# Two heads side by side on TensorE, and mask adds behind the first block, in a two-block transformer kernel

## The chip, the cores and the metric

One core of a Trainium2 chip. The metric is the device time of one execution in microseconds, as the median of several runs. Engines: TensorE (PE, matmul), VectorE (DVE), ScalarE (ACT), GpSimd (POOL) and SyncE (SP, which here only issues DMAs).

## What is computed

Two blocks of a decoder at a batch of 1, a sequence of 256 and a width of 1024, in fp32. Block 1 has two layers; each mixes with dilated attention (three groups of four heads of 64; the groups of a head slot are merged by their softmax denominators) and with stick-breaking attention, and then runs a convolution FFN of width 2816:

```python
h = rms_norm(x, norm_mix[l]); proj = h @ w_in[l]
sc = jnp.einsum('bqhd,bqkhd->bhqk', qg, kg) * scale        # dilated, per group, masked
p = jnp.exp(sc - m); o = jnp.einsum('bhqk,bqkhd->bqhd', p, vg) / den
...
up = h @ w_up; a, bval = up[..., :D_FF], up[..., D_FF:]
a = causal_depthwise_conv(a, conv_w) + conv_b
x = x + (jax.nn.silu(a) * bval) @ w_down
```

Block 2 has a layer with an even mixer (differential attention, and sparse attention that an indexer's scores select), one with an odd mixer (attention with sinks and a relative bias), cross-attention to a memory in both, and an MLP. The relative bias comes from a table of 32 buckets; some of the biases get a mask added.

## The kernel before, in words

Big matmuls (L231) take weights in two fp32r parts: SP loads a block of 512 KB of raw weights (L195, three buffers, up to five blocks ahead), ACT copies each half of it to the high part (L201), DVE subtracts to get the low part (L202), and PE multiplies in three terms. Every weight half on PE therefore needs one DVE instruction, which stands in DVE's queue among all the rest.

Attention runs in pairs of heads of 64, so that one head uses one half of the array. `dil_pair` (L721) takes one pair of head slots: the scores of three groups go to two banks, one per head (L734, buffers `sd`), once for the first 128 queries and in two banks for the second; DVE adds the mask and takes the maximum (L738); the transposed weights pass through PE and ACT (L749 to L754); and the values are summed over the groups into one bank, whose two halves belong to the two heads (L759 for the first 128 keys, L763 for the others, `pvd`). In block 2 `score_banks` (L580) makes the scores of two heads in two banks (L585, L586, `sc`), for the indexer, differential, sparse and odd-mixer pairs; `pv_pair` (L519) does their values (L524, L525, `pv`), for the odd mixer, the sparse pairs and the cross-attention.

The relative bias passes through DRAM: in the FFN of the first layer, seven copies of 768 KB (L654, buffer `skew_d`) are issued on POOL's queue, one for each step j = 2 to 8, paced by a small copy (L888) behind that step's product (L886). `bias_tile` (L489) loads a bias tile from there (L487, on POOL's queue, three buffers) and, where a mask is given, adds it on DVE (L494). The tiles are loaded as early as the pool lets them, long before block 2.

The order of instructions on each engine is decided by a scheduler that simulates the program when the kernel is built: it follows data, buffers and the `no_sync` edges. Such an edge says only that one instruction stands behind another in the order, and adds no semaphore.

Of the kernel before, what the change touches and what calls it, by code (L numbers as in the profile page):

```python
# [130 lines left out]
def net(ctx, tc, A, out):  # L131
# [86 lines left out]
    def hold(on):  # L218

        i = state["n"]  # L220
        if not on:
            state["limit"] = len(W)
            if i:
                ahead()
            return
        while i < len(W) and W[i][0] == W[state["n"]][0]:
            i += 1
        state["limit"] = i

# [259 lines left out]
    def bias_tile(heads, mask=None):  # L489
        t = sb("bias", "bias", (len(heads), T))  # L490
        for j, h in enumerate(heads):
            bias_load(t[:, j], h)
        if mask is not None:
            dve.tensor_tensor(t, t, mask[:, None, :].to_broadcast([P, len(heads), T]), op=OP.add)  # L494
        return t
# [5 lines left out]
    def lay_p(p, n1):  # L501
# [14 lines left out]
        act.activation(s1, t1, AF.Copy)  # L516
        return s0, s1

    def pv_pair(s0, s1, v, n1):  # L519

        o = bank("pv", "pv", (T,))
        for h in range(2):
            oo = o[h * 64:h * 64 + 64]
            pe.matmul(oo, v(h, 0), s0[:, h], start=True, stop=False, skip_group_check=True)  # L524
            pe.matmul(oo[:, T - n1:], v(h, 1), s1[:, h], start=False, stop=True, skip_group_check=True)  # L525
        return o
# [131 lines left out]
    for l in range(DEPTH):  # L658
# [62 lines left out]
        def dil_pair(hp):  # L721

            ps_p = []
            for i in range(2):
# [5 lines left out]
                for b, gs in enumerate(banks):  # L730
                    s = [bank("sc", "sd", (len(gs), n)) for _ in range(2)]
                    for g in gs:
                        for m in range(2):
                            pe.matmul(s[m][:, g - gs[0]], half(qT[g], hp, m)[:, col(i)], half(kT[g], hp, m)[:, :n],  # L734
                                      start=(g == gs[0]), stop=True, skip_group_check=True)
                    w = slice(gs[0], gs[-1] + 1)
                    for m in range(2):
                        dve.tensor_tensor_reduce(pv[m][:, w], s[m], m_dil[:, w, T - n:], 1.0,  # L738
                                                 mx[m][:, 0:1] if b else -3e38, op0=OP.add, op1=OP.max,
                                                 accum_out=mx[m][:, b:b + 1])  # L740
# [8 lines left out]
            for m in range(2):  # L749
                for dst, i, kt in ((t0[m][:, :, 0:P], 0, 0), (t0[m][:, :, P:T], 1, 0), (t1[m], 1, 1)):  # L750
# [89 lines left out]
        def residual(w, y, k, gains):  # L840
# [5 lines left out]
            def on_part(c, a, b):  # L846
# [3 lines left out]
                dve.tensor_tensor(t, x[c // 2][:, c % 2], a, op=OP.add)  # L850
# [90 lines left out]
    for j in range(2):  # L941
        dve.tensor_tensor_reduce(lprod, lamv[:, 2 * j], lamv[:, 2 * j + 1], 1.0, 0.0, op0=OP.mult, op1=OP.add,
                                 accum_out=lsum[:, j:j + 1])
# [79 lines left out]
    def even(h, nrm):  # L1023
# [48 lines left out]
        def index_scores(hp):  # L1072
            s = score_banks(lambda m: half(qi[hp // 2], hp % 2, m), lambda m: half(kc, 0, m))
            for hh in range(2):
                hd = 2 * hp + hh
                r = sb("ft", "relu", (384,))
                act.activation(r, s[hh], AF.Relu)
# [32 lines left out]
        def diff_pair(hp):  # L1110
            pl, dens = [], []
            for hh in range(2):
# [5 lines left out]
                for n, c in enumerate(COLS):  # L1118
                    m, i = n // 2, n % 2
                    dve.tensor_tensor_reduce(p[:, c], s[m][:, TILE[i]], bt[:, T - (i + 1) * P:], 1.0, -3e38,  # L1120
                                             op0=OP.add, op1=OP.max, accum_out=mx[:, n:n + 1])
# [30 lines left out]
        def dsa_pair(hp):  # L1152
# [10 lines left out]
            for n, c in enumerate(COLS):  # L1163
                dve.tensor_tensor_reduce(p[:, c], s[n // 2][:, TILE[n % 2]], bs[:, n // 2, TILE[n % 2]], 1.0, -3e38, op0=OP.add,  # L1164
                                         op1=OP.max, accum_out=mx[:, n:n + 1])
# [18 lines left out]
    def odd(h, nrm):  # L1184
# [22 lines left out]
        def pair(ch):  # L1207
# [7 lines left out]
            for n, cc in enumerate(cols):  # L1215
                m, i = n // 2, n % 2
                dve.tensor_tensor_reduce(p[:, cc], s[m][:, TILE[i]], bt[:, m, T - (i + 1) * P:], 1.0, -3e38,
                                         op0=OP.add, op1=OP.max, accum_out=mx[:, n:n + 1])
# [281 lines left out]
```

## Time and profile before

| | us |
|---|---|
| median of 3 runs | 1460.91 (1459.95 to 1466.13) |
| profiled execution | 1462.57 |
| its span on the core | 1460.5 |
| PE busy in the span | 1404.1 |
| DVE busy | 1015.4 |
| ACT busy | 886.0 |
| POOL busy | 34.2 |

The mean granted clock of PE was 0.988. The span is one execution of the profiled core; 2.1 us lie around it, and the execution is 1.66 us longer than the median. A row of PE's timeline is a run of instructions of one line: its start, its width, and in brackets the idle time before it and what released it. The small matmuls in fp32 leave two records each, so x4 in a row of them means two instructions. A row's end is modelled and may overlap the start of the next.

### The profile page before, as it was taken

To read this page: it belongs to the slowest core of one execution; us is meant where nothing else is said; L and a number is where in the kernel's file an instruction comes from. 1 tells how busy PE (TensorE), PEld (TensorE's weight loads), DVE (VectorE), ACT (ScalarE), POOL (GpSimd) and SP (SyncE) were. 2 spreads that over 40 slices of the span, in tenths; PEclk is the share of its full clock that TensorE was granted. 3 is DMA by queue.
4 is the path that set the end of the run, shared out by engine and by line. 5 is a ranking of instruction groups with operands and counts; after the bars stand their busy time and mean duration, and the time that the engine had idled before them with its cause. 6 is when DMAs were issued, how large, how long until landed. Compare 5 with 4: busy or idle time off the path is not lost.

```text
span 1460.5 us, 26250 instructions
## 1 busy us (share of the span) xinstructions
PE 1404.1 (96%) x9948; PEld 1274.4 (87%) x9948; DVE 1015.4 (70%) x2135; ACT 886.0 (61%) x1744; POOL 34.2 (2%) x63
## 2 busy tenths in 40 slices
PE   8999999799999999999999998899999999899997
PEld 6789999798888899999999987699989978699986
DVE  6555887567665659888867795687656876677554
ACT  7556665455565566666756656576656676576553
POOL 1000000100000000000000010000000010000000
PEclk9999999899999999999999999999999999999998
DMA  8533666576654345565665554156566534266662
GB/s 263 166 116 106 186 187 213 175 227 198 199 173 147 102 151 178 186 187 186 207 196 160 156 158 132 61 157 186 182 183 185 167 102 131 62 199 188 188 188 87
DMA packets 74447, 241.62 MB, mean 165 GB/s; under 512 B 11663, under 2 KB 16159, under 8 KB 74321
## 3 DMA queue, kind: packets, MB, share of 16 engines
q1 hardware_dynamic: 67568, 230.03, 50.8%
q0 software_dynamic: 6608, 9.74, 2.2%
q8 instruction: 78, 1.28, 0.4%
q14 instruction: 49, 0.39, 0.1%
q10 hardware_dynamic: 144, 0.19, 0.0%
HBM read 238.79 MB, written 6.60 MB: 168 GB/s over the span
## 4 chain that ended last, share of the span: by engine, by line
PE 85%; DMA 6%; DVE 4%; ACT 4%; issue 1%; SPq 0%; POOL 0%; DVEq 0%; ACTq 0%; POOLq 0%
PE mm L231 52%; PE mw L231 21%; DMA raw<-in_wt_dram 4%; PE ssum L427 2%; PE mo L231 1%; DVE w L202 1%; PE sd L734 1%; DMA skew_d<-brel_d 1%; ACT w L201 1%; PE pT L483 1%; PE pv L524 1%; PE sc L586 1%; PE sc L585 1%; PE pv L525 1%; PE pTd L483 1%
## 5 line engine op out<-in xcount | busy, mean ns | idle before, releaser
L202 DVE TENSOR_TENSOR w<-raw,w 128x512 fp32r<-128x512 f32 (+2 forms) x866 | 585.2, 685 | 336.2 <-ACT w L201 327.2
L201 ACT ACTIVATE w<-raw 128x512 fp32r<-128x512 f32 (+2 forms) x866 | 532.2, 625 | 424.4 <-PE mm L231 218.1
L231 PE MATMUL mm<-xh,w 128*128 128x256 f32 x5892 | 723.6, 283 | 20.5 <-DVE fa L885 13.4
L231 PEld LDWEIGHTS mm<-xh,w 128*128 128x128 f32 x5892 | 704.2, 189 | 37.4 <-issue 20.1
L231 PE MATMUL mw<-xh,w 128*128 128x512 f32 (+1 forms) x1832 | 329.3, 340 | 4.6 <-DVE mx L1164 2.5
L231 PEld LDWEIGHTS mw<-xh,w 128*128 128x128 f32 x1832 | 282.1, 189 | 47.7 <-DVE mx L1164 2.9
L231 PE MATMUL mm<-w,xh 128*128 128x512 f32 (+2 forms) x672 | 147.1, 372 | 7.2 <-ACT w L201 7.1
L231 PEld LDWEIGHTS mm<-w,xh 128*128 128x128 f32 x672 | 114.0, 191 | 30.7 <-ACT w L201 8.1
L978 ACT ACTIVATE xh<-x,vec 128x256 fp32r<-128x256 f32 x48 | 22.6, 501 | 11.5 <-DVE x L1333 11.0
L487 POOL DMA_DIRECT2D bias<-skew_d x28 | 15.1, 543 | 611.7 <-DVE nm L535 275.0
L880 ACT ACTIVATE ftt<-fa,vec 128x256 f32<-128x256 f32 x44 | 24.1, 595 | 8.1 <-DVE fa L875 6.9
L231 PE MATMUL mo<-xh,w 128*128 128x256 f32 x192 | 28.0, 288 | 0.5 <-ACT xh L498 0.5
L231 PEld LDWEIGHTS mo<-xh,w 128*128 128x128 f32 x192 | 24.4, 189 | 3.8 <-issue 1.2
L981 DVE SCALAR_TENSOR_TENSOR xh<-x,vec,xh 128x256 fp32r<-128x256 f32 x48 | 22.0, 480 | 1.1 <-ACT xh L978 1.1
L431 ACT ACTIVATE sq<-x 128x512 f32<-128x512 f32 x33 | 20.4, 618 | 2.4 <-DMA x<-in_xT_dram 2.1
L881 DVE SCALAR_TENSOR_TENSOR ftt<-fa,vec,ftt 128x255 f32<-128x255 f32 x44 | 20.9, 483 | 0.7
L882 DVE SCALAR_TENSOR_TENSOR ftt<-fa,vec,ftt 128x254 f32<-128x254 f32 x44 | 21.0, 477 | 0.0
L178 ACT ACTIVATE ftt<-ftt 128x512 f32<-128x512 f32 x22 | 13.9, 631 | 9.9 <-DVE ftt L882 9.9
L265 ACT ACTIVATE xh<-fa 128x512 fp32r<-128x512 f32 x22 | 13.7, 625 | 9.9 <-DVE fa L886 9.8
L734 PE MATMUL sd<-qTs 64*128 64x128 f32 (+1 forms) x96 | 18.8, 350 | 0.0
L438 DVE TENSOR_TENSOR sq<-sq 128x512 f32<-128x512 f32 x26 | 17.8, 686 | 0.0
L1332 DVE TENSOR_TENSOR y<-y,rstd 128x512 f32<-128x512 f32 (+1 forms) x25 | 14.5, 581 | 4.5 <-ACT rstd L178 4.4
(406 smaller groups left out, 1162.6 us busy)
## 6 DMA issues: line engine op xcount, KB each, us to landing
raw<-in_wt_dram SPq DMA_DIRECT2D x411, 512.0 KB, 3.6
raw<-in_wt_dram SPq DMA_DIRECT2D x16, 384.0 KB, 3.5
skew_d<-brel_d POOLq DMA_DIRECT2D x7, 768.0 KB, 16.2
bias<-skew_d POOLq DMA_DIRECT2D x28, 128.0 KB, 3.1
raw<-in_wt_dram SPq DMA_DIRECT2D x4, 520.0 KB, 3.5
mem<-in_memT_dram SPq DMA_DIRECT2D x8, 256.0 KB, 3.7
x<-in_xT_dram SPq DMA_DIRECT2D x4, 256.0 KB, 5.9
raw<-in_wt_dram SPq DMA_DIRECT2D x4, 256.0 KB, 3.4
```

Source lines behind the costliest of these rows:

```text
L201: act.activation(w[:, 0], raw[:, a:b], AF.Copy)
L202: dve.tensor_tensor(w[:, 1], raw[:, a:b], f(w[:, 0]), op=OP.subtract)
L231: i = pe.matmul(o, a, b, start=start, stop=stop, skip_group_check=True).ins
L427: state["sum"] = pe.matmul(self.ps, ones, s, start=first, stop=last).ins
L431: act.activation(sq, src, AF.Square)
L483: pe.transpose(o, i, ident)
L734: pe.matmul(s[m][:, g - gs[0]], half(qT[g], hp, m)[:, col(i)], half(kT[g], hp, m)[:, :n], start=(g == gs[0]), stop=True, skip_group_check= ...
L880: act.activation(t[:, c], a[:, c], AF.Identity, bias=vcol(vb + V_CB + ch), scale=w[2])
L881: dve.scalar_tensor_tensor(t[:, c, 1:], a[:, c, :T - 1], w[1], t[:, c, 1:], op0=OP.mult, op1=OP.add)
L882: dve.scalar_tensor_tensor(t[:, c, 2:], a[:, c, :T - 2], w[0], t[:, c, 2:], op0=OP.mult, op1=OP.add)
L978: act.activation(hi, t, AF.Copy, scale=g)
L981: return dve.scalar_tensor_tensor(lo, t, g, f(hi), op0=OP.mult, op1=OP.subtract)
```

## The change

Three things, all of them edges for the scheduler and an order in the code:

- `score_banks` and the scores of `dil_pair`: the matmuls of both heads stand behind the instructions that read both banks the last time (`readers["sc"]`), and the code alternates between the heads.
- `pv_pair` and the first values of `dil_pair`: both heads' matmuls stand behind the last ACT copy of the transposed weights, and `pv_pair` alternates between the heads.
- The mask adds L494, the products L942 and the copies L953 of block 2 stand behind the last residual add of block 1 (L850, `state["block1"]`).

```diff
+    readers = {"sc": [], "pT": []}
+
+    def behind(i, tag):
+
+        for p in readers[tag]:
+            no_sync(i, p)
...
         if mask is not None:
-            dve.tensor_tensor(t, t, mask[:, None, :].to_broadcast([P, len(heads), T]), op=OP.add)
+            no_sync(dve.tensor_tensor(t, t, mask[:, None, :].to_broadcast([P, len(heads), T]), op=OP.add).ins,
+                    state["block1"])
...
-        act.activation(s1, t1, AF.Copy)
+        readers["pT"] = [act.activation(s1, t1, AF.Copy).ins]
...
         for h in range(2):
-            oo = o[h * 64:h * 64 + 64]
-            pe.matmul(oo, v(h, 0), s0[:, h], start=True, stop=False, skip_group_check=True)
-            pe.matmul(oo[:, T - n1:], v(h, 1), s1[:, h], start=False, stop=True, skip_group_check=True)
+            behind(pe.matmul(o[h * 64:h * 64 + 64], v(h, 0), s0[:, h], start=True, stop=False,
+                             skip_group_check=True).ins, "pT")
+        for h in range(2):
+            pe.matmul(o[h * 64:h * 64 + 64, T - n1:], v(h, 1), s1[:, h], start=False, stop=True,
+                      skip_group_check=True)
...
-        s = []
+        s = [bank("sc", "sc", (384,)) for _ in range(2)]
         for h in range(2):
-            o = bank("sc", "sc", (384,))
-            pe.matmul(o[:, 0:P], q(h)[:, 0:P], k(h)[:, 0:P], start=True, stop=True, skip_group_check=True)
-            pe.matmul(o[:, P:], q(h)[:, P:], k(h), start=False, stop=True, skip_group_check=True)
-            s.append(o)
+            behind(pe.matmul(s[h][:, 0:P], q(h)[:, 0:P], k(h)[:, 0:P], start=True, stop=True,
+                             skip_group_check=True).ins, "sc")
+        for h in range(2):
+            behind(pe.matmul(s[h][:, P:], q(h)[:, P:], k(h), start=False, stop=True, skip_group_check=True).ins, "sc")
+        readers["sc"] = []
...
                         for m in range(2):
-                            pe.matmul(s[m][:, g - gs[0]], half(qT[g], hp, m)[:, col(i)], half(kT[g], hp, m)[:, :n],
-                                      start=(g == gs[0]), stop=True, skip_group_check=True)
+                            j = pe.matmul(s[m][:, g - gs[0]], half(qT[g], hp, m)[:, col(i)], half(kT[g], hp, m)[:, :n],
+                                          start=(g == gs[0]), stop=True, skip_group_check=True).ins
+                            behind(j, "sc")
...
-                    act.activation(dst, pt, AF.Copy)
+                    laid = act.activation(dst, pt, AF.Copy).ins
...
-                    pe.matmul(o[m * 64:m * 64 + 64], vn[g][:, 0, (2 * hp + m) * 64:(2 * hp + m) * 64 + 64],
-                              t0[m][:, g], start=(g == 0), stop=False, skip_group_check=True)
+                    no_sync(pe.matmul(o[m * 64:m * 64 + 64], vn[g][:, 0, (2 * hp + m) * 64:(2 * hp + m) * 64 + 64],
+                                      t0[m][:, g], start=(g == 0), stop=False, skip_group_check=True).ins, laid)
...
-                dve.tensor_tensor(t, x[c // 2][:, c % 2], a, op=OP.add)
+                state["block1"] = dve.tensor_tensor(t, x[c // 2][:, c % 2], a, op=OP.add).ins
...
-            dve.tensor_copy(sink4[:, :, 2 * m + i], sink[:, 8 * m:8 * m + 8])
+            no_sync(dve.tensor_copy(sink4[:, :, 2 * m + i], sink[:, 8 * m:8 * m + 8]).ins, state["block1"])
```

L942 gets the same edge as L953. In the places that read the banks (L738, ACT's relu of the indexer, and the mask-and-maximum of the differential, sparse and odd-mixer pairs) the instructions are put into `readers["sc"]`.

How the scheduler's order moves is shown at three places. The numbers of lines after the change are some 7 to 12 higher: L734, L759 and L763 become L745, L771 and L775; L494, L885, L850, L942 and L953 become L501, L897, L862, L954 and L965; L231 becomes L238.

PE, first dilated pair of layer 0 (`pvd_979` its values, `sd_951` and `sd_952` the second score bank of its two heads, `pd0`/`pd1` the transposed weights of the heads, `mm` big matmuls), before:

```order
L759 MATMUL pvd_979<-pd0_819,vnat_813 64x256
L763 MATMUL pvd_979<-pd1_820,vnat_666 64x128
L231 MATMUL mm_994<-xh_132,w23_775 128x256 x4
L231 MATMUL mm_994<-xh_137,w23_778 128x256 x10
L763 MATMUL pvd_979<-pd1_821,vnat_666 64x128
L734 MATMUL sd_951<-qTs_322,qTs_443 128x256
L734 MATMUL sd_951<-qTs_322,qTs_564 128x256
L763 MATMUL pvd_979<-pd1_820,vnat_666 64x128
L734 MATMUL sd_952<-qTs_322,qTs_443 128x256
L734 MATMUL sd_952<-qTs_322,qTs_564 128x256
L763 MATMUL pvd_979<-pd1_821,vnat_666 64x128
L763 MATMUL pvd_979<-pd1_820,vnat_813 64x128
```

The same place after the change:

```order
L771 MATMUL pvd_979<-pd0_819,vnat_666 64x256
L745 MATMUL sd_951<-qTs_322,qTs_443 128x256
L745 MATMUL sd_951<-qTs_322,qTs_564 128x256
L745 MATMUL sd_952<-qTs_322,qTs_443 128x256
L745 MATMUL sd_952<-qTs_322,qTs_564 128x256
L771 MATMUL pvd_979<-pd0_818,vnat_813 64x256
L771 MATMUL pvd_979<-pd0_819,vnat_813 64x256
L775 MATMUL pvd_979<-pd1_820,vnat_666 64x128
L775 MATMUL pvd_979<-pd1_821,vnat_666 64x128
L775 MATMUL pvd_979<-pd1_820,vnat_666 64x128
L775 MATMUL pvd_979<-pd1_821,vnat_666 64x128
L775 MATMUL pvd_979<-pd1_820,vnat_813 64x128
```

The scores of the two heads, which had a value matmul between them and others around them, now follow one another, and the values stand in two groups around them (four of the first kind stand just above the piece).

PE, one odd-mixer pair (`sc_13275` and the bank behind it its two heads, `pT0`/`pT1` transposes of another pair, `pv_13262` that pair's values), before:

```order
L585 MATMUL sc_13275<-kv_13009,qo_13011 128x128
L586 MATMUL sc_13275<-kv_13009,qo_13011 128x256
L483 MATMUL pT0_13139<-ident_106,po_13087 128x128 x2
L483 MATMUL pT1_13146<-ident_106,po_13087 128x128
L483 MATMUL pT0_13139<-ident_106,po_13087 128x128 x2
L483 MATMUL pT1_13146<-ident_106,po_13087 128x128
L585 MATMUL sc_13278<-kv_13009,qo_13011 128x128
L586 MATMUL sc_13278<-kv_13009,qo_13011 128x256
L524 MATMUL pv_13262<-pT0s_13144,kv_13009 64x256
L525 MATMUL pv_13262<-pT1s_13149,kv_13009 64x128
```

The same place after the change:

```order
L490 MATMUL pT1_13146<-ident_106,po_13087 128x128
L238 MATMUL mm_13319<-xh_12789,w354_13023 128x256 x4
L594 MATMUL sc_13275<-kv_13009,qo_13011 128x128
L597 MATMUL sc_13275<-kv_13009,qo_13011 128x256
L594 MATMUL sc_13276<-kv_13009,qo_13011 128x128
L597 MATMUL sc_13276<-kv_13009,qo_13011 128x256
L594 MATMUL sc_13391<-kv_13009,qo_13216 128x128
L597 MATMUL sc_13391<-kv_13009,qo_13216 128x256
```

This pair's heads now stand next to each other (128, 256, 128, 256 columns, not alternating by head); the first head of the next pair, `sc_13391`, stands behind them and its second head further on.

DVE, in the FFN of the first layer (`w` weight halves, `fa` and `ftt` the FFN's tiles), before:

```order
L882 SCALAR_TENSOR_TENSOR ftt<-fa,vec,ftt 128x254 [waits DVE_49]
L202 TENSOR_TENSOR w_2939<-raw_2934,w_2939 128x512 [waits Activation_49]
L494 TENSOR_TENSOR bias<-bias,m_chunk 128x256 [waits DMASW4_49,DMASW2_49]
L202 TENSOR_TENSOR w_2979<-raw_2977,w_2979 128x512 [waits DMAHW1_49,Activation_49]
L494 TENSOR_TENSOR bias<-bias,m_chunk 128x256 [waits DMASW5_49]
L885 TENSOR_TENSOR fa<-mm,rstd 128x512 [waits DVE_49,PE_49]
```

After the change, DVE at the end of block 1:

```order
L862 TENSOR_TENSOR x_8473<-x_6286,mm 128x256 [waits PE_49]
L954 ISA lp,ls<-lamv 128x64 [waits DMASW6_49]
L954 ISA ls 128x1
L965 COPY sink_8640<-sink 128x8 [waits DMASW5_49]
L965 COPY sink_8640<-sink 128x8 x3
L501 TENSOR_TENSOR bias<-bias,m_chunk 128x256 [waits DMASW4_49,DMASW2_49]
L501 TENSOR_TENSOR bias<-bias,m_chunk 128x256 [waits DMASW5_49]
L501 TENSOR_TENSOR bias<-bias,m_chunk 128x256 [waits DMASW2_49]
L202 TENSOR_TENSOR w_8578<-raw_8573,w_8578 128x512 [waits Activation_49]
```

The two mask adds have left their place in the FFN, where `ftt`, weight halves and L897 follow one another, and stand behind the last residual add with a third one, the two products (the second a little later) and the four copies; the weight half `w_8578` came directly behind the residual add before.

## Rows read from the trace of the kernel before

**Rows 1.** The page: busy us by engine, and the chain that ended last.

```profile
PE 1404.1 (96%) x9948; PEld 1274.4 (87%) x9948; DVE 1015.4 (70%) x2135; ACT 886.0 (61%) x1744; POOL 34.2 (2%) x63
...
PE 85%; DMA 6%; DVE 4%; ACT 4%; issue 1%; SPq 0%; POOL 0%; DVEq 0%; ACTq 0%; POOLq 0%
```

**Rows 2.** Waits on DVE: who waited for whom, us in total, times, longest.

```profile
DVE bias L494 <- DMA bias<-skew_d: 16.0, 4, 12.1
...
DVE pd L738 <- PE sd L734: 7.3, 10, 1.2
```

**Rows 3.** Waits on PE, the same columns.

```profile
PE mm L231 <- DVE fa L885: 13.4, 3, 10.4
...
PE mw L231 <- DVE mx L1164: 2.5, 1, 2.5
```

**Rows 4.** Timeline of DVE: start, width in us, what, idle before in brackets.

```profile
263.34 0.69 DVE L202 TENSOR_TENSOR w<-raw,w 128x512 fp32r<-128x512 f32 x1
276.14 0.42 DVE L494 TENSOR_TENSOR bias<-bias,m_chunk 128x256 f32<-128x256 f32 x1 [12.11 <-DMA bias<-skew_d]
```

**Rows 5.** Timeline of PE at the same place.

```profile
278.25 2.05 PE L231 MATMUL mm<-xh,w 128*128 128x256 f32 x8 [10.42 <-DVE fa L885]
```

**Rows 6.** Chain of waits, 255 to 300 us: start, us, what.

```profile
256.41 16.90 DMA skew_d<-brel_d
...
273.60 2.45 DMA bias<-skew_d
```

**Rows 7.** Stretches: us, busy PE, PEld, DVE, ACT, POOL, clock, DMA share, GB/s.

```profile
250.00:260.00 10.00, 10.00 (x87) 10.00 (x86) 6.22 (x11) 4.71 (x8) 1.27 (x2) 1.00 0.69 215
270.00:280.00 10.00, 1.75 (x8) 1.78 (x9) 3.86 (x8) 0.66 (x2) 1.77 (x4) 0.58 0.16 49
280.00:290.00 10.00, 10.00 (x79) 10.00 (x78) 8.37 (x15) 4.93 (x9) 1.34 (x3) 0.90 0.79 247
```

**Rows 8.** Timeline of PE, dilated pairs of layer 0.

```profile
75.18 0.70 PE L734 MATMUL sd<-qTs 64*128 64x256 f32 x4
...
85.41 0.65 PE L759 MATMUL pvd<-pd,vnat 128*64 128x256 f32 x2
...
88.84 1.29 PE L759 MATMUL pvd<-pd,vnat 128*64 128x256 f32 x9
...
89.97 0.38 PE L759 MATMUL pvd<-pd,vnat 128*64 128x256 f32 x1
...
92.14 0.43 PE L763 MATMUL pvd<-pd,vnat 128*64 128x128 f32 x2
92.50 1.13 PE L734 MATMUL sd<-qTs 64*128 64x256 f32 x4
...
94.98 0.65 PE L763 MATMUL pvd<-pd,vnat 128*64 128x128 f32 x6
```

**Rows 9.** Timeline of PE, scores: two adjacent heads, then one alone.

```profile
797.52 0.50 PE L585 MATMUL sc<-qb 64*128 64x128 f32 x4
797.84 0.61 PE L586 MATMUL sc<-qb 64*128 64x256 f32 x4
...
1174.41 0.48 PE L585 MATMUL sc<-kv,qo 64*128 64x128 f32 x2
1174.73 0.59 PE L586 MATMUL sc<-kv,qo 64*128 64x256 f32 x2
```

**Rows 10.** Timeline of PE, lone first value matmuls: cross-attention, odd mixer.

```profile
932.06 1.12 PE L524 MATMUL pv<-pT0s,mv 128*64 128x256 f32 x2 [2.15 <-ACT pT0s L509]
...
1190.76 0.65 PE L524 MATMUL pv<-pT0s,kv 128*64 128x256 f32 x2
```

**Rows 11.** Groups by line on DVE: what, count, busy us, mean ns, idle before.

```profile
L494 DVE TENSOR_TENSOR bias<-bias,m_chunk 128x256 f32<-128x256 f32 x4 | 1.7, 424 | 15.0 <-DMA bias<-skew_d 14.6 <-DVE gate L693 0.4
...
L953 DVE COPY sink<-sink 128x8 f32<-128x8 f32 x4 | 0.4, 168 | 0.0
```

**Rows 12.** Timeline of DVE at the end of block 1.

```profile
769.96 0.49 DVE L1010 SCALAR_TENSOR_TENSOR x<-x,vec,rstd 128x256 f32<-128x256 f32 x1 [1.50 <-ACT rstd L178]
```

More of the change, by code (lines that the diff above doesn't have):

```diff
@@ L733, in dil_pair @@
                         for m in range(2):
-                            pe.matmul(s[m][:, g - gs[0]], half(qT[g], hp, m)[:, col(i)], half(kT[g], hp, m)[:, :n],
-                                      start=(g == gs[0]), stop=True, skip_group_check=True)
+                            j = pe.matmul(s[m][:, g - gs[0]], half(qT[g], hp, m)[:, col(i)], half(kT[g], hp, m)[:, :n],
+                                          start=(g == gs[0]), stop=True, skip_group_check=True).ins
+                            behind(j, "sc")
                     w = slice(gs[0], gs[-1] + 1)
-                    for m in range(2):
+                    readers["sc"] = [
                         dve.tensor_tensor_reduce(pv[m][:, w], s[m], m_dil[:, w, T - n:], 1.0,
                                                  mx[m][:, 0:1] if b else -3e38, op0=OP.add, op1=OP.max,
-                                                 accum_out=mx[m][:, b:b + 1])
+                                                 accum_out=mx[m][:, b:b + 1]).ins for m in range(2)]
                 cols = [slice(0, 3 * n)]
@@ L941, in net @@
     for j in range(2):
-        dve.tensor_tensor_reduce(lprod, lamv[:, 2 * j], lamv[:, 2 * j + 1], 1.0, 0.0, op0=OP.mult, op1=OP.add,
-                                 accum_out=lsum[:, j:j + 1])
+        no_sync(dve.tensor_tensor_reduce(lprod, lamv[:, 2 * j], lamv[:, 2 * j + 1], 1.0, 0.0, op0=OP.mult,
+                                         op1=OP.add, accum_out=lsum[:, j:j + 1]).ins, state["block1"])
     actf(lsum, lsum, AF.Exp)
@@ L1076, in index_scores @@
                 r = sb("ft", "relu", (384,))
-                act.activation(r, s[hh], AF.Relu)
+                readers["sc"].append(act.activation(r, s[hh], AF.Relu).ins)
                 for i in range(2):
@@ L1119, in diff_pair @@
                     m, i = n // 2, n % 2
-                    dve.tensor_tensor_reduce(p[:, c], s[m][:, TILE[i]], bt[:, T - (i + 1) * P:], 1.0, -3e38,
-                                             op0=OP.add, op1=OP.max, accum_out=mx[:, n:n + 1])
+                    readers["sc"].append(dve.tensor_tensor_reduce(p[:, c], s[m][:, TILE[i]], bt[:, T - (i + 1) * P:], 1.0, -3e38,
+                                             op0=OP.add, op1=OP.max, accum_out=mx[:, n:n + 1]).ins)
                 dens.append(exps(p, mx, COLS))
@@ L1163, in dsa_pair @@
             for n, c in enumerate(COLS):
-                dve.tensor_tensor_reduce(p[:, c], s[n // 2][:, TILE[n % 2]], bs[:, n // 2, TILE[n % 2]], 1.0, -3e38, op0=OP.add,
-                                         op1=OP.max, accum_out=mx[:, n:n + 1])
+                readers["sc"].append(dve.tensor_tensor_reduce(p[:, c], s[n // 2][:, TILE[n % 2]], bs[:, n // 2, TILE[n % 2]], 1.0, -3e38, op0=OP.add,
+                                         op1=OP.max, accum_out=mx[:, n:n + 1]).ins)
             den = exps(p, mx, COLS)
@@ L1216, in pair @@
                 m, i = n // 2, n % 2
-                dve.tensor_tensor_reduce(p[:, cc], s[m][:, TILE[i]], bt[:, m, T - (i + 1) * P:], 1.0, -3e38,
-                                         op0=OP.add, op1=OP.max, accum_out=mx[:, n:n + 1])
+                readers["sc"].append(dve.tensor_tensor_reduce(p[:, cc], s[m][:, TILE[i]], bt[:, m, T - (i + 1) * P:], 1.0, -3e38,
+                                         op0=OP.add, op1=OP.max, accum_out=mx[:, n:n + 1]).ins)
             den = exps(p, mx, full, sinks=sink4[:, ch])
```

## The prediction

> **What bounds the kernel now.** I read the page's busy shares first: TensorE (PE) is busy for 1404.1 of 1460.5 us, and most of the chain that ended last lies on it [rows 1]. So PE's own work counts, and so does each of the few stalls that it has. The lists of waits then show the stalls. On VectorE (DVE) the mask add L494 waited 12.1 us once for a bias tile's DMA [rows 2]; on PE the largest sum of waits is 13.4 us for L885, and one of the three is 10.4 us long [rows 3]. The DVE and PE timelines put both at one place, 263 to 278 us, in the first layer's convolution FFN [rows 4, 5]: DVE had finished a weight half at 264.03 us, then stood on the mask add of a bias tile that nobody needs before block 2. The chain of waits there names the transfer: the skew copy took 16.90 us and the bias load behind it 2.45 us [rows 6]. Behind the mask add stood L202 and L885, for which PE waits. The table by stretches shows what it cost around it: in 270 to 280 us PE was busy for 1.75 us of 10, the DMA engines moved 49 GB/s, where they had moved 215, and the granted clock was 0.58 (a mean of the levels 2.4 and 1.2 GHz), and still 0.90 in the next stretch, with PE busy all the time [rows 7].
>
> Last I read PE's own timeline where the two heads of a pair run. The heads of a pair work on different halves of the array. The scores of both heads that stand next to each other in the order take 0.93 us from first to last (797.52 to 798.45), those of one head alone 0.91 us (1174.41 to 1175.32) [rows 9]: the second head is free where it is adjacent, and costs a whole run where it is not, already in the order of before, where the heads do not alternate. In the dilated pairs one matmul of 256 columns of each head takes 0.70 us, two of one head alone 1.13 us [rows 8].
>
> **Part 1, the pairing.** What is added are edges for the scheduler alone: no semaphore, no instruction. Its price is therefore what the order gains, run by run. Widths of neighbouring rows overlap a little (92.14 + 0.43 lies 0.07 behind 92.50 [rows 8]); I take 0.07 off each run.
> - First dilated pair, value matmuls (L759, L763) with the second score bank (L734) between them: seven runs now, of 0.65, 1.51 (88.84 to 90.35), 0.43, 1.13, 0.43, 1.13 and 0.65 us [rows 8] (the second runs of 0.43 and 1.13 are like the rows shown and follow at 93.56 and 93.92). They sum to 5.93, less 7 x 0.07 = 5.44 us. The new order has three runs. A further pair of 256 columns costs 1.13 - 0.70 = 0.43 us, a further pair of 128 columns 0.65 - 0.43 = 0.22 us at most. So 0.65 + 0.43 for the first, 0.70 + 0.43 for four scores, 0.65 + 3 x 0.22 for the last: 3.52, less 0.21 = 3.31 us. Gain 2.1 us.
> - First score bank of the same pair: two runs of 1.13 us become one: gain 1.06 us.
> - Second dilated pair: the lone first value matmul (one more run of 0.65 us, less 0.07) joins the rest, which grows by 0 to 0.43 us: gain 0.15 to 0.58, I take 0.4.
> That is 3.6 us a layer, and the order of layer 1 changes in the same way: **7.2 us**. PE waits for nothing in these stretches, so all of it is on the path.
> - Scores of block 2: of 20 pairs, 11 stand adjacent before and 12 after; one joins: 0.91 - 0.07 = **0.8 us**. Eight stay apart, because the scheduler fills between them with transposes and projections.
> - Value pairs of block 2: a lone first matmul costs 0.65 - 0.07 = 0.58 us [rows 10]. Two in the odd mixer and one in the even mixer join: **1.7 us**. In the cross-attentions three join; two of them ran at half clock, 1.05 us each (1.12 less 0.07) [rows 10], the third 0.58: 2.7 us. But these stand behind waits for ScalarE (2.15 us before the first), so the gain may only widen a wait; bounds 0 and 2.7, I take half, **1.3 us**.
> Part 1: 7.2 + 0.8 + 1.7 + 1.3 = **11.0 us**, between 8 (nothing from the cross-attentions, half of the other value pairs, the second dilated pair at 0.15) and 12.5 (nearly all of them).
>
> **Part 2, the mask adds.** They leave the queue in front of L202 and L885. The upper bound is PE's stall of 10.42 us [rows 5] and the clock behind it: from 278.25 to 280 us at about half, 0.9 us, and (1 - 0.90) x 10 = 1.0 us in the next stretch [rows 7]; 12.3 us. The lower bound is the DMA's: in the stalled stretch it fell short by (215 - 49) GB/s x 10 us = 1.66 MB, which takes 6.7 us at the 247 GB/s of the next stretch and 7.7 us at 215. If transfers are what PE would run into at once, only that comes back. PE was still fully busy at 215 GB/s [rows 7], so some supply is in store; I take **9 us**, nearer to the lower end since the supply has to last through four more skew copies (the one at 256.41 us is the third of the seven that the FFN's steps issue), and let the range of this term run from 5 to 12.3. GpSimd's queue keeps its order (loads of bias tiles and copies stay where they were, but for one late swap), so no transfer moves by itself.
>
> What was moved now stands at the end of block 1, between the last residual add and the weight half behind it: three mask adds of 0.42 us, four copies of 0.17 [rows 11], two products with their reads and two steps on their result, six small ones that I put at the copies' 0.17. That is 1.27 + 0.67 + 1.0 = 2.9 us. DVE now waits 1.50 us there for the norm's rstd [rows 12]; the rest, 1.4 us, is late for the first xh of block 2 and for one weight half. Bounds 0 (the program has projections of the memory ready for PE there, which need no x) and 2.9; I take **0.6 us**, as if these cover about half of the 1.4. The bias tiles landed long before, so nothing waits for DMA there.
>
> **Sum.** -11.0 - 9 + 0.6 = -19.4 us. On the profiled execution's own 1462.57 us this gives 1443.2; that execution is 1.66 us above the median of the runs, so against the median, 1460.91, **1441.5 us**. A measurement of this kernel tells some 0.5% (7.3 us) from no change.
>
> **Rivals.**
> 1. *The weight transfers take over the stall.* Without the stall the remaining four skew copies meet the weights with less supply in hand. For: the two other waits for L885, 13.4 - 10.4 = 3.0 us in all [rows 3], fall in the same layer. Against: DMA rates up to 247 GB/s were reached. Part 2 then gives 5 to 6.7 us instead of 9: about 1444.5 us.
> 2. *Adjacent in the order, but not side by side.* The second head of a dilated pair would wait for its bank or its copy and run alone as before; the change then does on PE what it says only in block 2. Part 1 gives 0.8 + 1.7 + 1.3 = 3.8 us: 1448.7 us. Against: PE hardly waits in that part, and both heads' inputs were ready together in the joined rows of before.
> 3. *Alternation itself pays.* Five of the score pairs that stood adjacent now alternate by head as well. If the order of before kept their heads one behind the other, each would gain 0.84 us: 4.2 us more, 1437.3 us. Against: the adjacent pair takes 0.93 us, and one head alone 0.91 [rows 9]; nothing is left to gain.
> The Trainium skill (TensorE: Matmul & The Clock Gate, What overlaps and what doesn't) says that matmuls start and end strictly in program order. By that rule rival 3 would hold; the trace of before disagrees, with 0.93 us for both heads against 0.91 for one.
> 4. *Slower: PE stands where it filled before.* While PE waited 10.4 us for L885 it ran nothing else [rows 5]: what stands behind a waiting instruction waits too. A lone head used to start once its own bank was read; now both stand behind the readers of both, with projections queued behind them. Place: 20 score pairs and 12 score-bank pairs of the dilated layers. It decides from a mean stall of 19.4/32 = 0.6 us (gain gone), and (19.4 + 7.3)/32 = 0.83 us makes it slower by 0.5%; at 1.0 us, 32 us in all, 1473.5 us. For: PE already waited up to 2.5 us for a mixer's softmax (L1164) [rows 3]. Against: such waits are few, DVE waits on PE's scores instead (7.3 us, 10 times [rows 2]), and the scheduler moved the pairs back behind other work rather than leave holes.
>
> **How the numbers follow.** My forecast 0.57, rival 1 0.17, rival 2 0.12, rival 3 0.04, rival 4 0.05; 0.05 for what I don't see (the scheduler reordered later parts slightly, the last MLP among them). The range reaches from 1433 us (part 1 at 12.5, part 2 at 12.3, boundary 0, which is 1436.1, and 3 us of rival 3 under it) to 1451 us (part 1 at 8, part 2 at 5, boundary 2.9, which is 1450.8), and holds rivals 1 and 2. Faster by over 0.5% is below 1453.6: nearly all of the forecast and rivals 1 to 3, 0.89; within 0.5% 0.07 (the tail of rival 2, part of the unseen); slower 0.04, nearly all rival 4.
>
> **What would show it.** Part 2: no wait of L494 for DMA in the list of DVE, PE's 10.4 us for L885 gone, PE near 10 of 10 from 260 to 280 us with the granted clock at 1.00, and the start of block 2 earlier by some 16 us. The waits for L885 and L201 that are left in that layer, above 3.0 us, price rival 1. Part 1: three rows of L759, L734 and L763 in place of seven, some 3.3 us in all; rival 2 would show a hole or a bracketed wait between the heads. The block's end: DVE's row before L1010 without a wait. I am wrong if the waits of PE on L738, L1164 or L1217 (the softmax readers of the pairs) grow by more than a few us, or if the first layer's FFN keeps its length.

## The result and the profile after

The changed kernel takes 1446.92 us (median of 4 runs, 1445.65 to 1448.74), the one before 1460.87 in the same comparison: a ratio of 0.990 with a 95% interval of 0.988 to 0.992, 14 us less. The prediction had 1441.5 in a range of 1433 to 1451. The profiled execution of the changed kernel took 1445.65 us with a span of 1443.5, 17.0 us less than the span before. The medians are 14 us apart and the profiles 17, because the profile before was 1.7 us above its median and this one 1.3 below.

Where the 17 us came from can be read from PE's timelines: the first matmul on the same weight block is looked up in both profiles, and the difference is followed through the program. One row per stretch, in us:

| stretch (times of the profile before) | difference at its end | what the stretch adds |
|---|---|---|
| start, to 34.8 | +0.7 | +0.7 |
| mixing of layer 0, to 216.5 | -3.8 | -4.5 |
| first FFN, to 282.8 | -15.2 | -11.4 |
| first FFN, rest, to 356.2 | -10.4 | +4.8 |
| mixing of layer 1, to 544.3 | -15.3 | -4.9 |
| end of block 1 and start of block 2, to 803.0 | -15.4 | -0.1 |
| block 2, to the last MLP at 1254.5 | -19.9 | -4.5 |
| last MLP, first blocks, to 1326.1 | -17.1 | +2.7 |
| end, 1446.9 | -17.0 | +0.1 |

So the dilated pairs gave 9.4 us, the first FFN gave 11.4 and took 4.8 back, the block boundary cost nothing, and block 2 gave 4.5 and took 2.7 back. The page of the changed kernel, busy time by engine and the chain that ended last by engine (answering to [rows 1]):

```profile
PE 1396.3 (97%) x9948; PEld 1275.8 (88%) x9948; DVE 1016.4 (70%) x2135; ACT 886.6 (61%) x1744; POOL 34.4 (2%) x63
...
PE 87%; DVE 4%; ACT 4%; DMA 4%; issue 1%; SPq 0%; DVEq 0%; ACTq 0%
```

PE is busy for 7.8 us less, and DMA has fallen from 6% of the chain to 4%. The waits on PE, in the columns of [rows 3]:

```profile
PE mm L238 <- ACT xh L990: 6.0, 4, 2.5
...
PE mm L238 <- DVE fa L897: 4.0, 3, 1.9
...
PE mm L238 <- DVE fa L887: 1.9, 1, 1.9
...
PE sc L594 <- DVE mx L1176: 1.0, 1, 1.0
...
PE sc L594 <- DVE mx L1229: 0.7, 1, 0.7
```

The wait for L885 (now L897) went from 13.4 us to 4.0, the longest from 10.4 to 1.9, but L875 (now L887) has 1.9 us that were not there. The last two rows are score banks (L585, now L594) that wait for the softmax readers of the pair before: L1164 (now L1176) of the sparse pairs, L1217 (now L1229) of the odd mixer. These waits in PE's timeline, where [rows 5] had the one of 10.42 us:

```profile
264.74 17.19 PE L238 MATMUL mm<-xh,w 128*128 128x256 f32 x144 [0.72 <-DVE fa L897]
283.83 18.81 PE L238 MATMUL mm<-xh,w 128*128 128x256 f32 x144 [1.90 <-DVE fa L887]
304.07 11.52 PE L238 MATMUL mm<-xh,w 128*128 128x256 f32 x96 [1.44 <-DVE fa L897]
317.47 7.44 PE L238 MATMUL mm<-xh,w 128*128 128x256 f32 x48 [1.88 <-DVE fa L897]
```

Four waits, 5.94 us in all, none of them behind a mask add: L494 is gone from the FFN. The stretches around them, columns as in [rows 7]:

```profile
260.00:270.00 10.00, 9.28 (x79) 9.10 (x79) 5.35 (x9) 3.98 (x7) 0.73 (x2) 1.00 0.56 186
270.00:280.00 10.00, 10.00 (x87) 9.90 (x86) 8.28 (x15) 5.61 (x10) 3.66 (x5) 1.00 0.77 243
...
285.00:290.00 5.00, 5.00 (x32) 5.00 (x32) 4.33 (x9) 2.52 (x5) 0.00 (x0) 0.69 0.87 266
315.00:320.00 5.00, 3.12 (x22) 2.95 (x22) 3.62 (x6) 2.82 (x5) 0.00 (x0) 0.89 0.53 187
320.00:325.00 5.00, 5.00 (x35) 4.95 (x35) 4.66 (x10) 3.07 (x6) 0.00 (x0) 0.77 0.61 198
```

The 10 us in which PE had been busy for 1.75 are now full. But behind two of the four waits the granted clock falls: 0.69 from 285 to 290, 0.89 and 0.77 from 315 to 325 us. Against 1.00 that is 1.6, 0.5 and 1.2 us, with PE busy nearly all the time but for the middle one: some 3.3 us, where before it was 1.9. What the waits stand behind is in the chain of waits of this stretch:

```profile
259.79 8.50 DMA raw<-in_wt_dram
...
274.00 7.64 DMA raw<-in_wt_dram
...
296.86 7.87 DMA raw<-in_wt_dram
```

These weight blocks took 7.6 to 8.5 us to land; the median over the whole kernel before was 3.6. Five of the seven skew copies were issued between 251.9 and 305.4 us (GpSimd's timeline).

The dilated pair of layer 0, and the same one of layer 1, in PE's timeline, where [rows 8] had seven runs:

```profile
90.39 1.08 PE L771 MATMUL pvd<-pd,vnat 128*64 128x256 f32 x8
91.40 1.14 PE L745 MATMUL sd<-qTs 64*128 64x256 f32 x8
92.47 0.65 PE L771 MATMUL pvd<-pd,vnat 128*64 128x256 f32 x4
...
466.11 1.08 PE L771 MATMUL pvd<-pd,vnat 128*64 128x256 f32 x8
467.12 1.14 PE L745 MATMUL sd<-qTs 64*128 64x256 f32 x8
468.19 0.65 PE L771 MATMUL pvd<-pd,vnat 128*64 128x256 f32 x4
468.68 0.82 PE L775 MATMUL pvd<-pd,vnat 128*64 128x128 f32 x12
```

Three runs, 1.08, 1.14 and then values to the end; in layer 1, from 466.11 to the end of the last row at 469.50, it is 3.39 us, less the 0.07 of overlap 3.32. The estimate was 3.31.

The end of block 1 on DVE, answering to [rows 12]:

```profile
751.92 0.41 DVE L862 TENSOR_TENSOR x<-x,mm 128x256 f32<-128x256 f32 x1
752.25 0.22 DVE L954 CUSTOM_DVE_ANT_0 lp<-lamv 128x64 f32<-128x64 f32 x1
752.39 0.08 DVE L954 DVE_READ_ACCUMULATOR2_ANT ls<- 128x1 f32 x1
752.39 0.39 DVE L965 COPY sink<-sink 128x8 f32<-128x8 f32 x4
752.68 1.09 DVE L501 TENSOR_TENSOR bias<-bias,m_chunk 128x256 f32<-128x256 f32 x3
753.69 0.69 DVE L202 TENSOR_TENSOR w<-raw,w 128x512 fp32r<-128x512 f32 x1
754.29 0.22 DVE L954 CUSTOM_DVE_ANT_0 lp<-lamv 128x64 f32<-128x64 f32 x1
754.44 0.08 DVE L954 DVE_READ_ACCUMULATOR2_ANT ls<- 128x1 f32 x1
754.59 0.49 DVE L1022 SCALAR_TENSOR_TENSOR x<-x,vec,rstd 128x256 f32<-128x256 f32 x1
```

The products, the copies and the three mask adds fill the hole, and L1010 (now L1022) comes without a wait, as was said. It starts 2.67 us behind the start of the last residual add (751.92 to 754.59), as it did before (767.29 to 769.96, the add being this row of before):

```profile
767.29 0.41 DVE L850 TENSOR_TENSOR x<-x,mm 128x256 f32<-128x256 f32 x1
```

The wait for rstd and the gaps around the weight half had covered all of it.

### The profile page after: what moved, and what is told of

Read it like the earlier page. It is cut to its first block, busy times and chain, and to the rows that moved or that the text cites. A ratio compares the mean times of both kernels' runs of the same rounds, so it can differ in the third digit from the quotient of the medians.

```text
span 1443.5 us, 26250 instructions
## 1 busy us (share of the span) xinstructions
PE 1396.3 (97%) x9948; PEld 1275.8 (88%) x9948; DVE 1016.4 (70%) x2135; ACT 886.6 (61%) x1744; POOL 34.4 (2%) x63
## 4 chain that ended last, share of the span: by engine, by line
PE 87%; DVE 4%; ACT 4%; DMA 4%; issue 1%; SPq 0%; DVEq 0%; ACTq 0%
PE mm L238 54%; PE mw L238 22%; DMA raw<-in_wt_dram 3%; PE mo L238 2%; PE ssum L434 2%; DVE w L202 1%; ACT w L201 1%; PE pT L490 1%; PE sd L745 1%; PE sc L597 1%; PE sc L594 1%; PE pv L531 1%; PE pTd L490 1%; ACT sq L438 1%; DMA x<-in_xT_dram 0%
## 5 line engine op out<-in xcount | busy, mean ns | idle before, releaser
L238 PE MATMUL mm<-xh,w 128*128 128x256 f32 x5892 | 729.0, 284 | 12.9 <-ACT xh L990 6.0
L238 PEld LDWEIGHTS mm<-xh,w 128*128 128x128 f32 x5892 | 709.3, 190 | 27.0 <-ACT w L201 8.3
L238 PE MATMUL mw<-xh,w 128*128 128x512 f32 (+1 forms) x1832 | 327.8, 339 | 2.0 <-DVE xh L273 1.5
L238 PEld LDWEIGHTS mw<-xh,w 128*128 128x128 f32 x1832 | 280.9, 188 | 44.7 <-DVE xh L273 2.1
L238 PE MATMUL mm<-w,xh 128*128 128x512 f32 (+2 forms) x672 | 146.4, 371 | 7.6 <-ACT w L201 6.9
L238 PEld LDWEIGHTS mm<-w,xh 128*128 128x128 f32 x672 | 113.9, 190 | 30.8 <-ACT w L201 7.7
L238 PE MATMUL mo<-xh,w 128*128 128x256 f32 x192 | 29.7, 303 | 0.5 <-ACT xh L506 0.5
L494 POOL DMA_DIRECT2D bias<-skew_d x28 | 15.1, 543 | 604.2 <-DVE nm L545 274.7
L238 PEld LDWEIGHTS mo<-xh,w 128*128 128x128 f32 x192 | 26.1, 203 | 3.5 <-ACT xh L506 1.3
L178 ACT ACTIVATE ftt<-ftt 128x512 f32<-128x512 f32 x22 | 13.9, 630 | 10.4 <-DVE ftt L894 10.4
L704 DVE TENSOR_TENSOR gate<-mm,rstd 128x512 f32<-128x512 f32 x16 | 11.1, 691 | 12.3 <-PE mm L238 12.2
L887 DVE TENSOR_TENSOR fa<-mm,rstd 128x512 f32<-128x512 f32 x22 | 15.2, 689 | 1.9 <-ACT rstd L178 1.2
## 6 DMA issues: line engine op xcount, KB each, us to landing
skew_d<-brel_d POOLq DMA_DIRECT2D x7, 768.0 KB, 15.2
```

What stands on the lines that cost most here:

```text
L238: i = pe.matmul(o, a, b, start=start, stop=stop, skip_group_check=True).ins
```

## The experiments

Each was timed side by side with the kernel before. "Ratio" compares all runs of a kernel with all runs of the kernel before, with its 95% interval; it can differ a little from the quotient of the two medians. The steps of the table above were read from each profile in the same way, and the two dilated layers gave -4.5 and -4.9 us in every kernel that has their pairing.

### The two halves, one at a time

The mask adds, products and copies behind block 1 and nothing else:

```diff
-            dve.tensor_tensor(t, t, mask[:, None, :].to_broadcast([P, len(heads), T]), op=OP.add)
+            no_sync(dve.tensor_tensor(t, t, mask[:, None, :].to_broadcast([P, len(heads), T]), op=OP.add).ins,
+                    state["block1"])
...
```

> The mask adds, products and copies behind block 1, pairing left out. My theory (the first FFN gets back the 10.4 us stall, but the weight transfers under the skew copies and the clock take a part of it back at once): the FFN ends 6 to 7 us earlier than before, the block boundary costs 0 to 0.6, so 1454 to 1455 us. The sum of my prediction has 9 - 0.6 = 8.4 us here, 1452.5. If the give-back in the FFN comes only because the pairing made PE early there, this kernel keeps nearly all of the 11.4 us: 1450.

Measured: 1453.98 us, ratio 0.9946 (0.9929 to 0.9963), 7.1 us less than the 1461.03 of before. In its profile the FFN gives 11.7 us and takes 3.6 back by 356 us, and these waits of PE are left (L885 is L886 here, L875 is L876):

```profile
PE mm L231 <- DVE fa L886: 3.0, 2, 2.5
...
PE mm L231 <- DVE fa L876: 2.4, 1, 2.4
```

So 5.4 us of waits are there without any pairing: the give-back does not hang on PE being early. The forecast's 8.4 us lies within the interval, which is 5.4 to 10.4 us.

The pairing and nothing else (the change, with L494, L942 and L953 as before):

> The pairing alone, the mask adds left where they were. Theory: both dilated layers give 4.5 and 4.8 us, block 2 1 to 2 us: 1449 to 1451 us, and the stall of 10 us in the first FFN is there. The sum of my prediction had 11.0: 1449.9. Rival (pairs wait at the heads of PE's queue): less than 5 us, with bracketed waits before score or value rows.

Measured: 1452.24 us, ratio 0.9936 (0.9910 to 0.9961), 8.8 us less by the medians and 1.2 above the upper end of the theory, which is within the spread of its runs. The rival's less than 5 us is out. The long wait is back, in the list of waits on PE (L885 is L896 here):

```profile
PE mm L238 <- DVE fa L896: 9.8, 3, 8.6
```

Only the dilated pairs (L734, L759 with their edges; `score_banks` and `pv_pair` as before):

> Only the dilated pairs' scores and values are put together. Theory: 9.3 us, 4.5 in layer 0 and 4.8 in layer 1: 1451.5 us. By my prediction's rows 7.2 us: 1453.7. Rival (adjacent but not side by side): under 2 us, 1459 or more.

Measured: 1452.24 us, ratio 0.9933 (0.9907 to 0.9960), 8.8 us less and the same as all of the pairing. By the timing alone both 9.3 and 7.2 us would do; the profile, with -4.5 and -4.9 us in the two layers, decides for the first. Rival 2, adjacent but not side by side, is out.

Only the pairs of block 2 (`score_banks`, `pv_pair` and their readers; `dil_pair` as before):

> Only block 2's score and value pairs are put together. Theory: what PE saves there is mostly lost again to half clock and waits at the ends of the cross-attentions: 0.5 to 2 us, 1459 to 1460.5. By my prediction's rows 3.8 us: 1457.1. If the loss seen at the second cross-attention is only where the changed kernel happens to stand, this gives over 3 us.

Measured: 1462.88 us, ratio 1.0006 (0.9992 to 1.0020): nothing that shows, and a gain of more than some 1.2 us is excluded, the prediction's 3.8 and the upper part of the theory with it. Its profile shows the gain and the loss: from 967 to 1254 us it gains 2.0 us on the kernel before, and at the start of the last MLP it loses 2.5. The granted clock there (columns as in [rows 7]). In this kernel:

```profile
1267.80:1272.80 5.00, 5.00 (x29) 5.00 (x30) 5.00 (x10) 3.05 (x7) 0.00 (x0) 0.66 0.00 0
```

In the kernel before:

```profile
1269.00:1274.00 5.00, 4.96 (x40) 4.81 (x41) 4.98 (x10) 3.50 (x8) 0.00 (x0) 1.00 0.00 0
```

Both are the first 5 us of the last MLP, behind a wait of some 2.5 us for xh (the normalised input of the MLP, written by ACT) in either kernel. In the first the clock falls behind that wait, to a mean of 0.66 (1.00 and 0.50 are the levels of 2.4 and 1.2 GHz); in the kernel before it stays at 1.00.

### Does the order of the heads matter

The changed kernel with the scores of block 2 head after head:

```diff
             behind(pe.matmul(s[h][:, 0:P], q(h)[:, 0:P], k(h)[:, 0:P], start=True, stop=True,
                              skip_group_check=True).ins, "sc")
-        for h in range(2):
             behind(pe.matmul(s[h][:, P:], q(h)[:, P:], k(h), start=False, stop=True, skip_group_check=True).ins, "sc")
```

> The changed kernel, with the scores of block 2 written head after head instead of alternating; the edges behind the readers stay. Theory (adjacent heads run side by side either way): no difference from the changed kernel beyond a us, 1446 to 1448. Rival 3 (alternation itself pays, 0.84 us for each of some five pairs): about 4 us more, 1451.

Measured: 1445.71 us, ratio 0.9896 (0.9879 to 0.9913), no slower than the changed kernel. The first score pair of block 2 in PE's timeline, alternating in the changed kernel:

```profile
782.14 0.49 PE L594 MATMUL sc<-qb 64*128 64x128 f32 x4
782.47 0.60 PE L597 MATMUL sc<-qb 64*128 64x256 f32 x4
```

and head after head in this one:

```profile
779.16 0.50 PE L594 MATMUL sc<-qb 64*128 64x128 f32 x4
779.48 0.61 PE L596 MATMUL sc<-qb 64*128 64x256 f32 x4
```

Both take 0.93 us from first to last, as the adjacent pair of before did [rows 9]. (That this one runs head after head is read from its code: the rows are sorted by start time and do not show the program's order.) By the Trainium skill's rule (TensorE: Matmul & The Clock Gate, What overlaps and what doesn't) that matmuls start and end strictly in program order, the second would be longer; the runs disagree. Rival 3, which gives 1451 us here, is out.

### What took the FFN's gain back

The changed kernel, with the skew copies at every second step of both FFNs:

```diff
-            if l == 0 and 2 <= j < 9:
+            if j in ((2, 4, 6, 8), (2, 4, 6))[l]:
                 pace = pool.tensor_copy(sb("sm", "pace", (1,)), a[:, 0, 0:1]).ins
-                no_sync(copy(4 * (j - 2)), pace)
+                no_sync(copy(4 * (j // 2 - 1 + 4 * l)), pace)
```

> The changed kernel, with the seven skew copies spread over the FFNs of both layers (four and three, at every second step) instead of seven in the first. Theory (skew copies and weights together ask more of the DMA than it gives, and this is what gave 4.8 us of the 11.4 back): the waits for L885 in the first FFN go to nearly none, clock 1.00 there, 4 to 5 us faster than the changed kernel: 1442 to 1443. Rival (DVE's or ACT's order makes those waits, not the DMA): they stay, 1446 to 1448.

Measured: 1438.42 us, ratio 0.9844 (0.9825 to 0.9864), 8.5 us less than the changed kernel and more than any of the expectations. The stretches of its first FFN:

```profile
260.00:270.00 10.00, 10.00 (x87) 10.00 (x86) 7.60 (x14) 6.44 (x12) 0.00 (x0) 1.00 0.63 204
...
280.00:290.00 10.00, 10.00 (x87) 10.00 (x86) 6.55 (x11) 4.88 (x9) 0.74 (x2) 1.00 0.70 220
...
300.00:310.00 10.00, 10.00 (x87) 10.00 (x86) 6.60 (x13) 4.70 (x9) 0.00 (x0) 1.00 0.67 234
```

PE is full in every one and the clock 1.00; no wait for L885 or L875 is left in the list. The copies on GpSimd's timeline stand 23 us apart:

```profile
250.00 1.11 POOL L665 DMA_DIRECT2D skew_d<-brel_d  x1
...
272.79 1.08 POOL L665 DMA_DIRECT2D skew_d<-brel_d  x1
...
296.46 1.12 POOL L665 DMA_DIRECT2D skew_d<-brel_d  x1
```

In the table's steps the first part of the FFN gives 12.3 us and the rest, which had taken 4.8 back, now gives 4.0 more, mostly the 3.0 us of other waits that the kernel before had there. The second FFN, which now has three copies, loses nothing.

The changed kernel with the copies in the mixing part of layer 1, behind its value and row projections:

```diff
+            if l == 1 and c0 in (2560, 2816, 3328, 3840, 4352):
+                paced(s[:, 0, 0:1])
...
+        def paced(t):
+            no_sync(copy(4 * brel_state.setdefault("n", 0)),
+                    pool.tensor_copy(sb("sm", "pace", (1,)), t).ins)
+            brel_state["n"] += 1
...
+            if l == 1:
+                paced(vn[-1][:, 0, 0:1])
...
-            if l == 0 and 2 <= j < 9:
-                pace = pool.tensor_copy(sb("sm", "pace", (1,)), a[:, 0, 0:1]).ins
-                no_sync(copy(4 * (j - 2)), pace)
```

> The changed kernel, with the seven skew copies paced by the mixing part of layer 1, where the core moves 120 GB/s, instead of by the first FFN. Theory (DMA contention in the first FFN): the FFN runs without waits for L885, and the leads of 15 to 25 us of the weights in the mixing part hide the copies: 4 to 6 us faster than the changed kernel, 1441 to 1443. Rival (the order of DVE makes the waits): no gain. If the copies slow the weights in layer 1 as they did in layer 0, the gain is lost there and shows as new waits between 440 and 530 us.

Measured: 1439.65 us, ratio 0.9855 (0.9839 to 0.9870). The first FFN gives the same 12.3 and 4.0 us; between 544 and 765 us of the kernel before it loses 2.8, and its list of waits on PE has one of 1.4 us, at 525 us, that the changed kernel has not:

```profile
PE mm L238 <- DVE gate L704: 1.4, 1, 1.4
```

The last of the copies was issued at 510 us and took 15.8, so it was still under way then and the transfers may be what costs there too; this was not tried by itself. Two different places for the copies, and both take the give-back away. The landing times of the weight blocks issued between 225 and 325 us go with that: a median of 7.0 us (at most 8.9) in the changed kernel, with seven copies in that time, 4.5 (at most 8.2) with four, and 3.8 (at most 5.6) with none. So it was the DMA, not the order on DVE. The Trainium skill (DMA: Bandwidth & Descriptors, Queues, rings and completion order) says that each DMA engine goes round its queues packet by packet; that agrees with weight blocks that mostly take 7 us and more beside a copy and some 3.6 without.

The kernel before with only the copies spread:

> The kernel before with only the skew copies spread over both FFNs. The mask adds keep their place in the first FFN, behind a bias load that waits for the third copy. Theory (two causes: the queue behind the mask add, and contention): the long wait of L494 stays at 8 to 12 us, one step pair later, while the 3.0 us of other waits for L885 go: 1456 to 1459. Rival (contention made the long wait too, and a copy alone lands in time): the wait goes as well, 1448 to 1450.

Measured: 1456.29 us, ratio 0.9972 (0.9956 to 0.9988). The long wait stays, one step pair later, and is shorter on PE; in the chain of waits:

```profile
277.68 14.77 DMA skew_d<-brel_d
...
292.74 2.39 DMA bias<-skew_d
```

and in the list of waits on PE:

```profile
PE mm L231 <- DVE fa L885: 6.8, 1, 6.8
```

The copy took 14.77 us where it had taken 16.90 [rows 6]: it lands late even with no other copy beside it (the one before it was issued at 254.8 us and took 15.7). The median is 4.9 us below that of the kernel before, as the theory had it. So there were two causes, the queue behind the mask add and the contention, and the change removes only the first.

### What block 2's pairing is worth

The dilated pairing and the mask adds, block 2's scores and values as before:

> The dilated pairing and the mask adds of the change, with block 2's scores and values as before. Theory (what block 2's pairing saves on PE, the clock takes back there): the same as the changed kernel within 1.5 us, 1445.5 to 1448.5. By my prediction's rows, which gave block 2 3.8 us, it would be 3.8 us slower: 1450.7.

Measured: 1444.86 us, ratio 0.9892 (0.9877 to 0.9908), not told apart from the changed kernel. In its profile the last MLP begins without a loss. The first 5 us of the MLP, behind the wait for xh, in the changed kernel and then in this one:

```profile
1250.20:1255.20 5.00, 4.98 (x29) 4.98 (x30) 5.00 (x10) 3.01 (x7) 0.00 (x0) 0.66 0.00 0
```

```profile
1251.10:1256.10 5.00, 5.00 (x40) 4.84 (x41) 5.00 (x10) 3.56 (x8) 0.00 (x0) 1.00 0.00 0
```

At the same place, 0.66 or 0.67 stands in the profiles of all seven kernels with block 2's pairing (the changed one, pairs only, block 2 only, heads in turn, copies spread, copies early, and the last one below), and 1.00 in the six without it (before, adds only, dilated only, copies spread alone, this one and the next). It is (1 - 0.66) x 5 = 1.7 us of the 2.1 to 2.8 that are lost there.

The same with the copies spread:

> Dilated pairing, mask adds behind block 1, skew copies spread over both FFNs; block 2's scores and values as before. Theory (block 2's pairing gives nothing that lasts): the same as the kernel with spread copies and all of the change, 1437 to 1439.5. If the saving of block 2's rows counts, 1441 to 1442.

Measured: 1437.48 us, ratio 0.9841 (0.9824 to 0.9859), the fastest median of all; it is not told apart from the kernel with spread copies and the whole change.

Spread copies and the whole change, but the cross-attentions' values in the order of before:

```diff
+        if n1 == T:
+            for h in range(2):
+                oo = o[h * 64:h * 64 + 64]
+                pe.matmul(oo, v(h, 0), s0[:, h], start=True, stop=False, skip_group_check=True)
+                pe.matmul(oo[:, T - n1:], v(h, 1), s1[:, h], start=False, stop=True, skip_group_check=True)
+            return o
```

> The change with spread skew copies, but the values of the cross-attentions (calls of pv_pair with two full key blocks) in the order of before. Theory (pairing the cross-attention's values is what lets the clock fall behind the wait for xh at the start of the last MLP): the clock of the 5 us behind that wait is 1.00 instead of 0.66, and the last MLP starts 2 us nearer to its place: about 1436.5, against 1438.4 with the cross-attentions paired. Rival (the clock falls for another reason: the odd mixer's pairing or the reordered start of the MLP): 0.66 stays there, 1438 to 1439.5.

Measured: 1438.64 us, ratio 0.9854 (0.9837 to 0.9870). The clock behind the wait for xh:

```profile
1240.90:1245.90 5.00, 5.00 (x30) 5.00 (x31) 5.00 (x11) 3.11 (x7) 0.00 (x0) 0.67 0.00 0
```

0.67, and 2.1 us are lost at the start of the last MLP as in the others: at that place the theory falls. It holds at another. The first MLP of block 2 (its first matmul is at 951.64 us in the kernel before) also begins behind a wait of 2.47 or 2.48 us for xh. Its first 5 us, with the copies spread and the whole change:

```profile
922.50:927.50 5.00, 4.99 (x29) 4.99 (x30) 5.00 (x10) 3.02 (x7) 0.00 (x0) 0.66 0.00 1
```

With the cross-attentions' values in the order of before:

```profile
924.30:929.30 5.00, 5.00 (x40) 4.83 (x41) 5.00 (x10) 3.57 (x8) 0.00 (x0) 1.00 0.00 0
```

So there it is the pairing of the cross-attention's values that lets the clock fall. The six kernels that have it, block 2 alone among them, have 0.66 to 0.68 at that place and lose 1.0 to 1.4 us between 945 and 967 us of the kernel before; the other seven have 1.00 and lose at most 0.2.

PE's own order behind the wait is the same in the kernels of both kinds for the first matmuls, and the wait is as long. What differs is how far behind the cross-attention it ends: the clock was at its lower level there, and from its rise to the end of the wait for xh pass 12.6 to 13.9 us at the thirteen places where it falls again, and 14.2 to 14.9 at the thirteen where it does not. No run moved that distance by itself, so this is not shown to be the cause. Which part of the odd mixer's or the sparse pairs' order makes it shorter at the last MLP stays open.

## Why the prediction was right, and where it was off

**Dilated pairs: 7.2 us said, 9.4 measured.** The mechanism was right and each joined run has the width that was worked out (3.32 against 3.31 us). What was too small is the term as a whole. The layer gave 4.5 to 4.9 us instead of 3.6; only the runs were priced, and not what lies between them, but the last 0.9 to 1.3 us were not taken apart.

**The mask adds: 9 us said, 6.6 in this profile, 7.1 (5.4 to 10.4 by the interval) when they moved alone.** Rival 1 came in part: PE gained 11.4 us at first and lost 4.8 again to waits behind weight blocks and to the clock behind these waits. In the profiles of three other kernels with the same FFN the first part gives 11.7, 12.2 and 11.1 us and the rest takes back 3.6, 2.7 and 2.7 (adds alone; heads in turn; dilated pairs and adds): 8.1, 9.5 and 8.4 us are left. So the step "some supply is in store, I take 9" lies within what the profiles give, and 6.6 is the lowest of four; whether the kernel or the execution makes that difference was not separated. The cause of the give-back was named rightly: with the copies elsewhere it is gone. The lower bound from the DMA was 6.7 us, which this profile misses by 0.1 and the others keep; the clock was priced for the stall that goes, and not for the new waits that come.

**The block boundary: 0.6 us said, 0 measured.** The 1.50 us of DVE's wait and the spare time of the first weight half covered all of the added work.

**Block 2: 3.8 us said (0.8, 1.7 and 1.3), nothing measured.** This is the term that failed. The profile has 2.0 us of gain from 967 to 1254 us, but alone the pairing gives a ratio of 1.0006 (0.9992 to 1.0020), and left out of the change it costs nothing. Half of the cross-attentions' gain was taken off for waits; what took the rest was the clock at the start of both MLPs (1.0 to 1.4 and 2.1 to 2.8 us lost there), places whose work the change does not touch and that the sum had no term for.

**The rivals.** Rival 1 came in part; rival 2 and rival 3 are out; rival 4 too: the list of waits on PE shows 0.7 us for the odd mixer's readers, 1.0 for the sparse pairs' as before (`PE sc L585 <- DVE mx L1164: 1.0, 1, 1.0` there), and none for the dilated layers' readers.

**The sum.** -19.4 us was said and -17.0 came in the profile, -14.0 in the medians. In the profile: 2.2 us more from the dilated pairs, 2.4 less from the FFN, 0.6 that the boundary did not cost, 2.0 less from block 2 (4.5 gained, 2.7 given back, against 3.8), and 0.7 lost at the start, where such differences come without a change too (the kernel with dilated pairs only lost 2.8 there). The even mixer's part of the 4.5 comes and goes without block 2's pairing: from 803 to 967 us, -1.9 in the changed kernel, -2.0 in the one with dilated pairs only, +0.2 in the one with block 2's alone. So the 1.8 us net for block 2 in this profile are not all the pairing's, and the timing of block 2 alone, which shows nothing, is the better measure. That the sum came within 5.5 us of the median is in part luck: what the dilated pairs gave beyond their term covered about half of what block 2 did not give.

## What to carry to other kernels

Two heads on two halves of the array run side by side as soon as they are adjacent in the order, in whatever order among themselves; look for split pairs, not for pairs that do not alternate. When a stall goes, look for what had been resting during it: here the transfers, whose copies then fell closer on each other, and spreading the copies brought another 8.5 us. A few us saved close to a place where PE waits anyway can be lost again to half clock behind that wait; count them only if a run shows them.

## What the runs showed of the hardware

The clock fell behind a wait of 1.9 us (0.69 for 5 us) and behind one of 2.5 us (0.66) in some orders, and stayed at 1.00 behind a wait of the same 2.47 us at the same place in others, the same way in every one of the thirteen profiles: at the last MLP it fell with block 2's pairing, and at the first with the pairing of the cross-attention's values. Copies of 768 KB within DRAM took some 14 to 17 us each, and beside them weight blocks of 512 KB mostly took 7 us and more to land, where the median of the kernel was 3.6. What the first FFN gives back differs by 2 us between four profiles, while the gain of the dilated pairs repeats to 0.03 us in every profile.
